# A two-layer hybrid decoder trunk: TensorE in traced order, and the weights' low parts subtracted on GpSimd

## The chip, the cores and the metric

The kernel runs on one core of one Trainium2 chip. Its time is device microseconds of one execution; the medians are of several runs. The profile is of one execution of the same program. TensorE (PE in the views) does matmuls and transposes, VectorE (DVE) and ScalarE (ACT) read and write both on-chip memories, GpSimd (POOL) works on SBUF, and SyncE (SP) issues most loads. Each engine runs its own instructions in one order; between engines they wait for each other through semaphores.

## The reference

The input `x` has 512 rows of 1024. Each of two layers normalises it, projects it with one wide matrix (1024 to 12388), runs five branches on the parts, gates each branch with a SiLU, projects each to 1024 columns, adds them under sigmoid gates and projects the sum once more:

```
xn = rms_norm(h, norm_g[l])
(a_q, a_k, a_v, i_q, i_k, i_w, b_cq, b_ckv, b_kr, c_q, c_k, c_v,
 d_u, d_v, e_q, gates, merge) = jnp.split(xn @ w_in[l], offsets, axis=-1)
branches = (dsa_branch(...), mla_branch(...), diff_branch(...), sgu_branch(...), memory_branch(...))
mixed = functools.reduce(jnp.add, [
    jax.nn.sigmoid(merge[:, :, n]) * ((o * jax.nn.silu(gates[:, :, n])) @ w_branch[l, n])
    for n, o in enumerate(branches)])
h = h + mixed @ w_out[l]
...
return rms_norm(h, final_norm_g)
```

Branch A attends to keys picked by an indexer, B is latent attention with a separate rotary key, C is differential attention (two softmaxes of half heads, one taken from the other), D is a causal spatial mixing in chunks of 128 rows after a layer norm, E attends to 256 memory rows. All is float32.

## The kernel before

**Weights.** All weights are float32 in HBM. A weight tile of 128x512 is loaded into one of four `raw` buffers by SyncE, two tiles to a load; ScalarE copies it to `wh` in a rounded type (line 374), and VectorE subtracts: `wl = raw - wh` (line 377, `split_steps`). There are 556 such tiles and five slots of `wh` and `wl`. Activations are split the same way (`split`, lines 191 and 192). Each product is then three matmuls, high by high, low by high and high by low (`three`, lines 459 to 461), so a tile of 512 columns takes twelve matmuls of 128x128 by 512.

**Order.** The program is traced by Python generators. `plan` lists the weight units in the order of a string, and between the matmuls of a unit `tick` moves on by some nanoseconds: it takes one step of splitting the next weights, and gives queued attention steps their turn when their delay has run out (`Pace`, with constants such as `LAG_QROPE` and `PACE`). What this emits is the traced order. The tile framework is called with `schedule_with_timeline_sim=True`: a scheduler then puts each engine's instructions in an order of its own, by a simulated timeline, with the traced order as priority, as long as the data dependencies hold.

**Where that order was tied by hand.** In the differential scores (`diff_attention`, line 1122) six matmuls belong together: three products for each of two halves of 64 rows. `behind` (line 180) adds a dependency without a semaphore from each to the one before it, which fixes the order of the six, but not that they stand next to one another.

**Names.** PSUM has three pools: four banks `m` (`pm` for the units, `pz` for branch D's spatial products), three banks `a` (`pa`, `pS` scores, `pT` and `pN` transposes, `pI` indexer) and one bank `o` (`po`). A bank is taken again once its last reader is done. `kh`, `kl`, `qh` and `ql` are the split keys and queries, filled by lines 191, 192 and, for the rotary rows of branch B, by copies at lines 916 and 917. `vnh` and `vnl` are the split output of the layer norm, a chain of VectorE instructions at lines 1210 to 1217. `z` (line 1239) is the activation that empties `pz`. `pth` and `ptl` are the split transposed probabilities.

**GpSimd** holds the mask and table building at the start, the small `pow` of each norm (line 250), the product of the spatial weights with the triangle (line 1184, four times) and a few loads.

Of the kernel before, what the change touches and what calls it, by code (L numbers as in the profile page):

```python
# [12 lines left out]
ALU = mybir.AluOpType  # L13
# [41 lines left out]
class Pace:  # L55


    def __init__(self):
        self.queues = {}
        self.later_ = []  # L60
        self.owner = {}
        self.now = 0.0
        self.busy = set()
# [69 lines left out]
def trunk(tc, d, out, taps=None):  # L133
    nc = tc.nc
    V, A, G, T = nc.vector, nc.scalar, nc.gpsimd, nc.tensor
    pace = Pace()
    PSUM = bass.MemoryType.PSUM
    stack = []

    def pool(name, bufs, **kw):  # L140
        p = tc.tile_pool(name=name, bufs=bufs, **kw)
        stack.append(p)
        return p.__enter__()
# [8 lines left out]
    smp = pool("small", 16)  # L152
    psp = pool("ps", 1, space=PSUM)
    drp = pool("scr", 1, space=bass.MemoryType.DRAM)
# [7 lines left out]
    def tr(dt=F32, name="tr"):  # L162
        return trp.tile([128, 512], dt, tag="tr", name=name)

    def small(n=1, name="sm"):
        return smp.tile([128, 8], F32, tag="sm", name=name)[:, :n]
# [4 lines left out]
    def psa(name="pa"):  # L171
        return psp.tile([128, 512], F32, tag="a", bufs=3, name=name)

    def pso(name="po"):
        return psp.tile([128, 512], F32, tag="o", bufs=1, name=name)

    def f32(ap):
        return ap.bitcast(F32)

    def behind(ins, prev):  # L180

        if prev is not None:
            tc.add_manual_dep(ins.ins, prev.ins.name, mybir.DependencyInfo(
                mybir.DependencyClass.NoSync, mybir.DependencyReason.DATA), reason="behind")
# [67 lines left out]
    def rstd_of(ss, n, eps, width, name="rstd"):  # L252
        r = small(n, name)
        V.tensor_scalar(r, ss, 1.0 / width, eps, op0=ALU.mult, op1=ALU.add)
        rsqrt(r, r)
        return r
# [95 lines left out]
    order, state = [], {"dma": 0, "split": 0, "slot": 0}  # L352
# [10 lines left out]
    def wtile():  # L363
        i = state["slot"] % NW
        state["slot"] += 1
        return [wp.tile([128, 512], F32R, tag=f"{n}{i}", bufs=1, name=n) for n in ("wh", "wl")]

    def split_steps(g):
        g.h, g.l = [], []
        for a in range(0, g.n, g.per):  # L370
            b = min(a + g.per, g.n)
            h, lo = (z.rearrange("p (k c) -> p k c", k=g.per) for z in wtile())
            raw, hv, lv = g.raw[:, a:b, :g.width], h[:, :b - a, :g.width], lo[:, :b - a, :g.width]
            A.activation(hv, raw, AF.Copy)  # L374
            g.h.append(h)
            yield
            V.tensor_tensor(out=lv, in0=raw, in1=f32(hv), op=ALU.subtract)  # L377
            g.l.append(lo)
            yield

# [165 lines left out]
    def softmax_head(ps, L, mask, scale):  # L546
        p = pp.tile([128, 512], F32, tag="p", name="p")
        m = small(1, "m")
        V.tensor_tensor_reduce(out=p[:, :L], in0=ps[:, :L], in1=mask, op0=ALU.add, op1=ALU.min,  # L549
                               scale=-scale, scalar=-GONE, accum_out=m)  # L550
        s = small(1, "s")
        A.activation(p[:, :L], p[:, :L], AF.Exp, bias=m, scale=-1.0, accum_out=s)  # L552
        return p, s
# [97 lines left out]
    def layer(l, mm):  # L651
# [457 lines left out]
        def diff_attention(hf):  # L1109
            sc = 64 ** -0.5  # L1110
            X = S[f"df{hf}"]

            def scores(e, i):
                L = 128 * (i + 1)
                N = max(256, L)
                q = slice(i * 128, i * 128 + 128)
                pss = [psa("pS") for _ in range(2)]
                rows = [slice(64 * s, 64 * s + 64) for s in range(2)]
                prev = None
                for n, (a, b) in enumerate(((0, 0), (0, 1), (1, 0))):  # L1120
                    for ps, r in zip(pss, rows):
                        mm = T.matmul(ps[:, :N], X["q"][e][a][r, q], X["k"][e][b][r, :N], start=n == 0, stop=n == 2)  # L1122
                        behind(mm, prev)
                        prev = mm
                return lambda: [softmax_head(ps, L, cm[:, 512 - 128 * i:640], sc) for ps in pss]

            def norm(ps_, e, i):
                L = 128 * (i + 1)
                (p0, s0), (p1, s1) = ps_
                r0, r1 = small(1, "r0"), small(1, "r1")  # L1130
                V.reciprocal(r0, s0)
                V.reciprocal(r1, s1)
                V.tensor_tensor(out=r1, in0=r1, in1=nlam[:, l:l + 1], op=ALU.mult)
                V.tensor_scalar(p1[:, :L], p1[:, :L], r1, None, op0=ALU.mult)
                V.scalar_tensor_tensor(out=p0[:, :L], in0=p0[:, :L], scalar=r0, in1=p1[:, :L],
                                       op0=ALU.mult, op1=ALU.add)

            def pv_rows(e, i):
                o = pso()
                for kb in range(i + 1):  # L1140
                    for part in range(2):
                        T.matmul(o[:, :256], pf[part][:, kb * 384 + i * 128:kb * 384 + i * 128 + 128],  # L1142
                                 X["v"][kb][:, e].rearrange("p z c -> p (z c)"),
                                 start=(kb == 0 and part == 0), stop=(kb == i and part == 1))
                on = X["o"].setdefault(e, [None] * 4)
                on[i] = rows = tr(name="don")
                A.activation(rows[:, 128:256], o[:, 128:256], AF.Copy)
                V.tensor_tensor(out=rows[:, :128], in0=o[:, :128], in1=rows[:, 128:256], op=ALU.add)
                ss = small(1, "dss")
                A.activation(rows[:, 128:256], rows[:, :128], AF.Square, accum_out=ss)  # L1150
                r = rstd_of(ss, 1, RMS_EPS, 128.0, "dr")
                V.tensor_scalar(rows[:, :128], rows[:, :128], r, None, op0=ALU.mult)

            def flip(e):
                p = psa("pN")
                for i in range(4):
                    T.transpose(p[:, i * 128:(i + 1) * 128], X["o"][e][i][:, :128], ident)
                oT["C"][2 * hf + e] = blk(F32, "oC")
                A.activation(oT["C"][2 * hf + e], p, AF.Copy, scale=dgain[:, l:l + 1])

            X["o"] = {}
            yield 2500.0
            yield from attend("C", causal_steps(range(2)), scores, norm,
                              lambda ps_, e, i: transposes(ps_[0][0], i), flip, pv_rows)

# [173 lines left out]
        for tok in ORDER.split():  # L1339
            c, a = tok[0], tok[1:]  # L1340
# [111 lines left out]
    mm = mm0 = {"rows": memt}  # L1452
    plan.append(lambda: None)
    for l in range(DEPTH):
        mm = layer(l, mm)
# [50 lines left out]
```

## Time and profile before

| | |
|---|---|
| median of 3 runs | 1822.18 us (1821.29 to 1822.37) |
| profiled execution | 1820.71 us, its span 1818.8 us |
| granted clock of TensorE | 0.993 on average |
| busy: TensorE, VectorE, ScalarE, GpSimd | 1769.3, 1158.0, 953.0, 65.7 us |
| instructions: TensorE, VectorE, ScalarE, GpSimd | 8793, 2801, 2143, 133 |

The span is from the first instruction to the last. Busy time counts work, not waiting. The list of waits of one engine says what each instruction waited for, how long in total and how often; the timeline of an engine gives the start of each instruction, its duration, and in brackets the idle time before it with what ended it. Rows of a matmul give about 0.39 us for 512 columns, though one begins about 0.23 us after another, because they overlap; the steps are therefore read from start to start.

### The profile page before, as it was taken

What the parts mean: (1) busy time and instruction counts of PE and PEld (TensorE: products, weight loads), DVE (VectorE), ACT (ScalarE), POOL (GpSimd) and SP (SyncE); (2) the same over time, 40 slices, a digit from 0 to 9 for tenths busy, and PEclk for the clock granted to TensorE, in tenths of its full rate; (3) what the DMA queues carried; (4) which work ended last, traced back from release to release, by engine and by line L of the source; (5) the groups of instructions that cost most, each with busy time, mean ns of one, the idle gap of its engine ahead of it and who ended that gap; (6) DMA issues with size and microseconds to landing.
All of it is one profiled execution on the core that took longest, in us unless ns stands there. A gap on an engine that the chain in (4) does not pass through costs nothing.

```text
span 1818.8 us, 24673 instructions
## 1 busy us (share of the span) xinstructions
PE 1769.3 (97%) x8793; PEld 1467.0 (81%) x8793; DVE 1158.0 (64%) x2801; ACT 953.0 (52%) x2143; POOL 65.7 (4%) x133
## 2 busy tenths in 40 slices
PE   7999999999989999999999999999999899999998
PEld 6877788877778888888987878788777788888887
DVE  7549776676786656445466497667767856554544
ACT  7447766444445665234355477564444556552333
POOL 1000000001010000000000000000010100000000
PEclk9999999999999999999999999999999999999999
DMA  7222221323223222343352322223232232223332
GB/s 237 76 70 62 69 77 58 94 81 100 63 81 93 79 73 82 93 126 93 121 172 58 76 62 76 82 59 93 70 104 70 59 93 70 70 84 105 113 127 70
DMA packets 151587, 161.00 MB, mean 89 GB/s; under 512 B 26293, under 2 KB 130793, under 8 KB 151465
## 3 DMA queue, kind: packets, MB, share of 16 engines
q1 hardware_dynamic: 148520, 149.21, 28.4%
q0 software_dynamic: 2944, 10.23, 1.7%
q8 instruction: 69, 1.13, 0.3%
q14 instruction: 54, 0.43, 0.1%
HBM read 155.22 MB, written 4.19 MB: 88 GB/s over the span
## 4 chain that ended last, share of the span: by engine, by line
PE 94%; DVE 4%; ACT 1%; issue 1%; DMA 0%; SPq 0%; POOL 0%; POOLq 0%; DVEq 0%; ACTq 0%
PE pm L459 27%; PE pm L460 27%; PE pm L461 27%; PE pT L567 2%; PE po L577 2%; PE pS L1122 2%; PE po L1142 1%; DVE wl L377 1%; PE pS L461 1%; PE pa L1026 1%; PE pS L460 1%; PE pS L459 1%; PE pa L532 1%; PE pS L1055 1%; PE pS L1054 1%
## 5 line engine op out<-in xcount | busy, mean ns | idle before, releaser
L377 DVE TENSOR_TENSOR wl<-raw,wh 128x512 fp32r<-128x512 f32 x556 | 376.9, 684 | 362.6 <-ACT wh L374 340.0
L374 ACT ACTIVATE wh<-raw 128x512 fp32r<-128x512 f32 x556 | 345.4, 625 | 445.9 <-PE pm L460 267.9
L459 PE MATMUL pm<-xh,wh 128*128 128x512 f32 x1040 | 414.6, 399 | 3.2 <-ACT nat L1019 2.3
L460 PE MATMUL pm<-xl,wh 128*128 128x512 f32 x1040 | 408.6, 393 | 0.0
L461 PE MATMUL pm<-xh,wl 128*128 128x512 f32 x1040 | 407.9, 393 | 0.0
L459 PEld LDWEIGHTS pm<-xh,wh 128*128 128x128 f32 x1040 | 195.9, 188 | 44.3 <-ACT nat L1019 2.7
L461 PEld LDWEIGHTS pm<-xh,wl 128*128 128x128 f32 x1040 | 195.7, 188 | 41.1 <-issue 0.7
L460 PEld LDWEIGHTS pm<-xl,wh 128*128 128x128 f32 x1040 | 195.9, 188 | 36.5 <-issue 0.5
L460 PE MATMUL pm<-wl,xh 128*128 128x512 f32 x512 | 202.0, 395 | 0.0
L461 PE MATMUL pm<-wh,xl 128*128 128x512 f32 x512 | 200.8, 394 | 0.0
L459 PE MATMUL pm<-wh,xh 128*128 128x512 f32 x512 | 200.5, 399 | 0.0
L552 ACT ACTIVATE p<-p,m 128x512 f32<-128x512 f32 (+1 forms) x192 | 107.1, 558 | 90.3 <-DVE m L549 89.9
L459 PE MATMUL pm<-yh,wh 128*128 128x512 f32 x320 | 125.5, 394 | 1.6 <-DVE acc L1311 1.6
L460 PE MATMUL pm<-yl,wh 128*128 128x512 f32 x320 | 126.2, 394 | 0.0
L461 PE MATMUL pm<-yh,wl 128*128 128x512 f32 x320 | 125.5, 393 | 0.0
L459 PEld LDWEIGHTS pm<-wh,xh 128*128 128x128 f32 x512 | 96.5, 188 | 20.3 <-ACT mth L1300 0.7
L461 PEld LDWEIGHTS pm<-wh,xl 128*128 128x128 f32 x512 | 96.4, 188 | 19.7
L460 PEld LDWEIGHTS pm<-wl,xh 128*128 128x128 f32 x512 | 96.6, 189 | 18.6 <-issue 0.5
L192 DVE TENSOR_TENSOR ptl<-pT,pth 128x512 fp32r<-128x512 f32 (+3 forms) x176 | 88.6, 504 | 30.8 <-ACT pth L191 29.7
L191 ACT ACTIVATE pth<-pT 128x512 fp32r<-128x512 f32 (+3 forms) x176 | 78.5, 448 | 53.6 <-PE po L577 33.5
L549 DVE CUSTOM_DVE_ANT_0 p<-pS,cm 128x128 f32<-128x128 f32 (+3 forms) x144 | 65.2, 464 | 50.3 <-PE pS L461 31.3
L558 ACT ACTIVATE p<-p,r 128x512 f32<-128x512 f32 (+3 forms) x128 | 71.4, 558 | 19.8 <-DVE r L557 19.3
(342 smaller groups left out, 2878.0 us busy)
## 6 DMA issues: line engine op xcount, KB each, us to landing
raw<-w_in SPq DMA_DIRECT2D x176, 512.0 KB, 3.7
raw<-w_branch SPq DMA_DIRECT2D x40, 512.0 KB, 3.5
raw<-w_in SPq DMA_DIRECT2D x36, 256.0 KB, 3.0
raw<-mem_w_kv SPq DMA_DIRECT2D x16, 512.0 KB, 4.9
raw<-w_out SPq DMA_DIRECT2D x16, 512.0 KB, 3.8
raw<-mla_w_uq SPq DMA_DIRECT2D x18, 128.0 KB, 2.7
xrow<-x SPq DMA_DIRECT2D x4, 512.0 KB, 7.3
raw<-mla_w_ukv SPq DMA_DIRECT2D x16, 128.0 KB, 2.5
```

The lines of the kernel that those rows point to most:

```text
L191: A.activation(hi, src, AF.Copy)
L192: V.tensor_tensor(out=lo, in0=src, in1=f32(hi), op=ALU.subtract)
L374: A.activation(hv, raw, AF.Copy)
L377: V.tensor_tensor(out=lv, in0=raw, in1=f32(hv), op=ALU.subtract)
L459: T.matmul(o, ah, bh, start=st, stop=False)
L460: T.matmul(o, ah, bl, start=False, stop=False)
L461: T.matmul(o, al, bh, start=False, stop=sp)
L549: V.tensor_tensor_reduce(out=p[:, :L], in0=ps[:, :L], in1=mask, op0=ALU.add, op1=ALU.min, scale=-scale, scalar=-GONE, accum_out=m)
L552: A.activation(p[:, :L], p[:, :L], AF.Exp, bias=m, scale=-1.0, accum_out=s)
L558: A.activation(p[:, :L], p[:, :L], AF.Copy, scale=r)
L567: T.transpose(ps[:, kb * 128:(kb + 1) * 128], p[:, kb * 128:(kb + 1) * 128], ident)
L577: T.matmul(o[:, q0:], v, pf[part][:, kb * 384 + q0:kb * 384 + 512], start=(kb == 0 and n == 0), stop=(kb == 3 and n == len(ts) - 1))
```

## The change

A class `InOrder` takes the place of `nc.tensor`: `matmul` and `transpose` go through it, and each instruction is given a dependency without a semaphore on the one issued before it. The scheduler can then no longer move any TensorE instruction past another: TensorE's order is the traced one. The other engines are still ordered by the scheduler. The pair order in `diff_attention` by `behind` is dropped. In `split_steps` the subtraction moves from VectorE to GpSimd; its operands are the same. In the changed file the matmuls and transposes all have the lines 152 and 155, of the class, and other lines are 21 higher.

```diff
+    class InOrder:
+        def __init__(self):
+            self.last = None
+
+        def _chain(self, ins):
+            if self.last is not None:
+                tc.add_manual_dep(ins.ins, self.last.ins.name, mybir.DependencyInfo(
+                    mybir.DependencyClass.NoSync, mybir.DependencyReason.DATA), reason="in order")
+            self.last = ins
+            return ins
+
+        def matmul(self, *a, **k):
+            return self._chain(nc.tensor.matmul(*a, **k))
+
+        def transpose(self, *a, **k):
+            return self._chain(nc.tensor.transpose(*a, **k))
+
+    T = InOrder()
...
             A.activation(hv, raw, AF.Copy)
             g.h.append(h)
             yield
-            V.tensor_tensor(out=lv, in0=raw, in1=f32(hv), op=ALU.subtract)
+            G.tensor_tensor(out=lv, in0=raw, in1=f32(hv), op=ALU.subtract)
...
-                prev = None
                 for n, (a, b) in enumerate(((0, 0), (0, 1), (1, 0))):
                     for ps, r in zip(pss, rows):
                         mm = T.matmul(ps[:, :N], X["q"][e][a][r, q], X["k"][e][b][r, :N], start=n == 0, stop=n == 2)
-                        behind(mm, prev)
-                        prev = mm
```

The number of matmuls and of vector instructions stays; 556 instructions go from VectorE's queue to GpSimd's. Three places of TensorE's order show what the chain does.

The first is the latent attention's keys in layer 1, near 178 us: `pm_1976` is the second bank of keys, `pm_2022` and `pm_2023` hold the values, and `pm_2070` and `pm_2071` are the next unit, which takes the keys' banks. TensorE before, at the first use of `pm_2071`:

```order
L461 MATMUL pm_2070<-xh4_119,wl_2080 128x512
L459 MATMUL pm_2070<-xh5_120,wh_2079 128x512
L460 MATMUL pm_2070<-xl5_128,wh_2079 128x512
L461 MATMUL pm_2070<-xh5_120,wl_2080 128x512
L459 MATMUL pm_2070<-xh6_121,wh_2092 128x512
L460 MATMUL pm_2070<-xl6_129,wh_2092 128x512
L461 MATMUL pm_2070<-xh6_121,wl_2093 128x512
L459 MATMUL pm_2071<-xh0_115,wh_2029 128x512
```

The same place now:

```order
L152 MATMUL pm_2023<-wh_1982,ckvl_1608 128x256
L152 MATMUL pm_2070<-xh0_115,wh_2029 128x512
L152 MATMUL pm_2070<-xl0_123,wh_2029 128x512
L152 MATMUL pm_2070<-xh0_115,wl_2030 128x512
L152 MATMUL pm_2071<-xh0_115,wh_2029 128x512
L152 MATMUL pm_2071<-xl0_123,wh_2029 128x512
L152 MATMUL pm_2071<-xh0_115,wl_2030 128x512
L152 MATMUL pm_2070<-xh1_116,wh_2029 128x512
```

Before, seven products of `pm_2070` (21 matmuls) came ahead of the first of `pm_2071`; now the two banks take turns, and one product (three matmuls) does.

The second is branch D's spatial products, near 543 us; `pN` is the transpose of branch C's output. TensorE before:

```order
L461 MATMUL pz_5844<-vnh_5556,wsl_5320 128x256
L460 MATMUL pz_5855<-vnl_5558,wsh_5319 128x256
L461 MATMUL pz_5855<-vnh_5556,wsl_5320 128x256
L459 MATMUL pz_5866<-vnh_5557,wsh_5336 128x256
L1157 MATMUL pN_5764<-ident_95,don_5721 128x128
```

And now:

```order
L152 MATMUL pz_5855<-vnh_5556,wsl_5320 128x256
L152 MATMUL pz_5866<-vnh_5557,wsh_5336 128x256
L152 MATMUL pz_5866<-vnl_5559,wsh_5336 128x256
L152 MATMUL pz_5866<-vnh_5557,wsl_5337 128x256
L152 MATMUL pz_5866<-vnh_5557,wsh_5336 128x256
```

The banks were begun one after another, with transposes in between; now each bank's two halves follow each other, the 24 matmuls of four banks in a row.

The third is one group of differential scores, `pS_4016` and `pS_4017`. TensorE before:

```order
L1122 MATMUL pS_4016<-kh_3732,qh_3702 128x384
L459 MATMUL pm_3962<-xh0_115,wh_3906 128x512
L460 MATMUL pm_3962<-xl0_123,wh_3906 128x512
L461 MATMUL pm_3962<-xh0_115,wl_3907 128x512
L459 MATMUL pm_3962<-xh1_116,wh_3906 128x512
```

And now:

```order
L152 MATMUL pS_4016<-kh_3732,qh_3702 128x384
L152 MATMUL pS_4017<-kh_3732,qh_3702 128x384
L152 MATMUL pS_4016<-kl_3733,qh_3702 128x384
L152 MATMUL pS_4017<-kl_3733,qh_3702 128x384
L152 MATMUL pS_4016<-kh_3732,ql_3703 128x384
L152 MATMUL pS_4017<-kh_3732,ql_3703 128x384
```

Before, the first matmul stood alone, 22 weight matmuls ahead of its five partners; now the six follow one another.

## Rows read from the trace of the kernel before

**Rows 1.** The page: busy time of each engine; then the chain by engine.
```profile
PE 1769.3 (97%) x8793; PEld 1467.0 (81%) x8793; DVE 1158.0 (64%) x2801; ACT 953.0 (52%) x2143; POOL 65.7 (4%) x133
...
PE 94%; DVE 4%; ACT 1%; issue 1%; DMA 0%; SPq 0%; POOL 0%; POOLq 0%; DVEq 0%; ACTq 0%
```

**Rows 2.** The page's groups: line, engine, operation; busy us, mean ns; idle before, releaser.
```profile
L377 DVE TENSOR_TENSOR wl<-raw,wh 128x512 fp32r<-128x512 f32 x556 | 376.9, 684 | 362.6 <-ACT wh L374 340.0
L374 ACT ACTIVATE wh<-raw 128x512 fp32r<-128x512 f32 x556 | 345.4, 625 | 445.9 <-PE pm L460 267.9
```

**Rows 3.** Waits of TensorE: waiting tile, releaser: us in total, times, longest.
```profile
PE pz L459 <- ACT vnh L191: 11.2, 2, 5.6
PE pa L231 <- DMA vec<-mla_kv_norm_g: 6.7, 1, 6.7
PE po L459 <- ACT pth L191: 3.5, 4, 1.5
PE pI L996 <- DVE iqs L969: 3.3, 2, 1.6
...
PE pm L459 <- DVE kl L192: 0.9, 1, 0.9
```

**Rows 4.** Busy us by stretch; columns: stretch, length, engines with instructions, clock, DMA.
```profile
170.00:192.00 22.00, 19.23 (x95) 15.07 (x94) 20.97 (x44) 20.68 (x43) 0.00 (x0) 1.00 0.22 55
...
530.00:553.00 23.00, 17.27 (x91) 14.96 (x90) 22.17 (x65) 14.02 (x38) 3.27 (x5) 0.85 0.20 58
```

**Rows 5.** Timeline of TensorE, near 375 and near 479: start, duration, line, instruction.
```profile
374.85 0.39 PE L460 MATMUL pm<-xl,wh 128*128 128x512 f32 x1
375.07 0.39 PE L461 MATMUL pm<-xh,wl 128*128 128x512 f32 x1
375.39 0.38 PE L1122 MATMUL pS<-kh,qh 64*128 64x256 f32 x1
375.70 0.50 PE L459 MATMUL pm<-xh,wh 128*128 128x512 f32 x1
...
479.13 0.39 PE L461 MATMUL pm<-yh,wl 128*128 128x512 f32 x1
479.45 0.38 PE L1122 MATMUL pS<-kh,qh 64*128 64x256 f32 x2
...
480.00 0.39 PE L1142 MATMUL po<-dv,pth 128*128 128x256 f32 x1
```

**Rows 6.** Timeline of GpSimd, two products that follow each other.
```profile
448.26 2.61 POOL L1184 TENSOR_TENSOR wsr<-wsr,tril 128x512 f32<-128x512 f32 x2 [3.37 <-DMA wsr<-sgu_w]
```

**Rows 7.** Timeline of VectorE in the same microseconds.
```profile
448.38 1.31 DVE L316 TENSOR_TENSOR rope<-nat,sP 128x64 f32<-128x64 f32 x1
...
449.69 0.67 DVE L1012 MATCH_REPLACE8 score<-m,score 128x512 f32<-128x512 f32 x1
450.28 0.74 DVE L318 TENSOR_TENSOR nat<-rope 128x128 f32<-128x128 f32 x1
```

**Rows 8.** Line 316, all of one shape: shortest, middle and longest in ns.
```profile
L316 DVE TENSOR_TENSOR rope<-nat,sP x24: 205/214/1306, 328.4 to 1447.5; 128x64 f32<-128x64 f32 x24
```

**Rows 9.** Timeline of ScalarE at the latent attention's keys.
```profile
182.40 0.58 ACT L191 ACTIVATE kh<-pm 64x512 fp32r<-64x512 f32 x1
183.01 0.63 ACT L916 ACTIVATE kh<-krh 32x512 fp32r<-32x512 f32 x1
...
188.31 0.62 ACT L374 ACTIVATE wh<-raw 128x512 fp32r<-128x512 f32 x1
```

**Rows 10.** Timeline of TensorE at branch D's spatial products.
```profile
542.79 0.79 PE L459 MATMUL pz<-vnh,wsh 128*128 128x256 f32 x2 [5.58 <-ACT vnh L191]
...
546.54 0.28 PE L461 MATMUL pz<-vnh,wsl 128*128 128x256 f32 x1
546.66 0.28 PE L459 MATMUL pz<-vnh,wsh 128*128 128x256 f32 x1
```

**Rows 11.** Timeline of ScalarE behind them.
```profile
544.57 1.22 ACT L1239 ACTIVATE z<-pz,cols 128x128 f32<-128x128 f32 x4 [0.80 <-PE pz L461]
```

## The prediction

> **What bounds the kernel now.** I read the engines' busy times first: TensorE is busy 1769.3 of 1818.8 us, VectorE 64%, ScalarE 52%, GpSimd 4%, and the chain of work that ended last is TensorE for 94% of its length [rows 1]. So no engine but TensorE can be shortened to any effect, and the question is only what TensorE's idle time becomes: 1818.8 - 1769.3 = 49.5 us, of which the list of its waits names 42.2 us, the sum of its 19 rows, and about 7 us lie behind its last matmul. The largest rows are few [rows 3]: 11.2 us in two waits for `vnh` ahead of the spatial matmuls of branch D, 6.7 us for a load at the start, 3.5 us for `pth`, 3.3 us for `iqs`, 0.9 us for `kl`. About 10 us of the 42 lie in the first 50 us and are not touched. The rest, some 32 us, come in a few places of each layer, where the other engines are full: in the 22 us from 170, VectorE is busy 20.97 and ScalarE 20.68 [rows 4]; in the 23 us from 530, VectorE 22.17. Elsewhere TensorE never waits.
>
> In the profiled execution 1820.71 us passed, 1.9 more than its span; the median of the runs, 1822.18, is 1.5 above it. I add changes to the profiled run and 1.5 at the end.
>
> **The differential scores become contiguous: a gain.** Six matmuls on 64 rows make up a group; two of them, on the two halves of the rows, run side by side. In a whole group of width 256, the matmul before starts at 479.13, the group at 479.45 and the next at 480.00 [rows 5]: 0.55 us for six, two at a time. In 18 of the 32 groups the scheduler leaves the first alone among the weights' matmuls and the other five later. The lone one has nothing beside it: the weight matmul before starts at 375.07, the lone one at 375.39, the next at 375.70 [rows 5]. Instead of one interval of 0.22 to 0.23 (374.85 to 375.07) there pass 0.63, so it costs 0.40, and the five left behind take as long as six do. In the new order all 32 groups stand whole: 18 x 0.40 = -7.2 us. Removing `behind` costs nothing, as the chain holds the same pairs.
>
> **VectorE loses the 556 subtractions**, 376.9 us [rows 2]. VectorE bounds nothing over the span, so this is worth only what TensorE waits for it; ScalarE's copies of 345.4 us [rows 2] stay, so of ScalarE's queue nothing goes.
>
> **GpSimd gets them.** The nearest row is its product over the same 128x512 in float32: two of them took 2.61 us, 1.31 each [rows 6]; that it writes another type here I can't see. 556 x 1.31 = 728 us, 40% of the span. It has to keep up with TensorE: a tile's twelve matmuls take 12 x 0.229 = 2.75 us, so up to twice that price GpSimd is hidden by the tile prepared ahead, and a wait for `wl` costs nothing. SyncE's raw buffers come free about 0.6 us later per tile, under four buffers; loads have that much in hand. Also the `pow` instructions and a few DMA issues of GpSimd stand behind a subtraction of at most 1.3 us; I put them at nothing beside the lags of 4 us that the source gives them.
>
> **But GpSimd and VectorE hold each other up.** While that product ran (448.26 to 449.61), a VectorE product of two SBUF inputs that takes 0.214 in the middle took 1.31, and the next one 0.74, while MATCH_REPLACE8 with one input took its usual 0.67 beside it [rows 6 to 8]. With GpSimd at work 40% of the time, such a VectorE instruction meets one under way 4 times in 10 and waits half of 1.31: 0.40 x 0.65 = 0.26 us on average. That matters where VectorE's queue is on TensorE's path, and there each layer has four places with some 15 to 20 such instructions between the event that starts the queue and the one TensorE waits for: at 0.28 each 5 us a place, 43 us in all eight; at 0.15 19 us; at nothing 0. I take 13, nearer to the low end, because the subtraction can just as well wait for VectorE, and the same queues are 40% of a subtraction shorter per tile.
>
> The Trainium skill, "SBUF — State Buffer", section "SBUF: two separate sides", says that the port pair is an exclusive lock between GpSimd and VectorE operations with two SBUF inputs, held for the whole instruction, and the loser blocks. By it every such meeting costs its full rest, which is the 43 us; rows 7 agree for two inputs and for one.
>
> **The order.** Today a scheduler moves whatever can run into TensorE's gaps. From now on a matmul that waits holds all behind it. I went through the new order and compared, for each pair of a TensorE result and the first matmul that needs its evacuation, the time of TensorE's instructions between the two (0.228 us per 512 columns [rows 5], 0.12 per 256 [rows 10]) with the sum of the queue in between. The same sum for the old order gives 48.8 us where about 43 are seen, so it leans high by some 6.
> - The MLA keys, near 178. Old: the first matmul of `pm_2071`, which needs the keys' bank, had 21 matmuls of `pm_2070`, the scores and the indexer ahead of it. New: three of `pm_1976`, 24 of 256 columns and three of `pm_2070`: 6 x 0.228 + 24 x 0.119 = 4.2 us. ScalarE has to do 13 instructions there, 4 of `kh` at 0.58, 6 copies of the rotary part at about 0.62, two weight copies at 0.62 and one more [rows 9]: 7.9 us. 3.7 us are waited where 0.9 is now [rows 3]; the rotary part of q ahead of it adds up to 2.3. Together +5 a layer.
> - The merge between 212 and 264: ScalarE's 25 instructions from a `pth` to the last `qh`, 14.6 us, over TensorE's 10.6; with smaller waits beside it +4.5 a layer.
> - Branch D, 530 to 550. Old: 5.58 us [rows 10]. The 24 spatial matmuls stood mixed with the transposes of C and A. New: in a row. A tile's second three waits for the two activations of its first half, four of which took 1.22 [rows 11]. Each of four tiles so costs 1.2 to 1.5, near 5.5; ahead of them the queue of VectorE (47 instructions, 16.4 us without subtractions) over TensorE's 13.9 and the handing over leaves 3.1. 8.6 for 6.2: +2.5.
> - The memory branch near 100: 2.4 us of matmuls now stand between `pth` and its use where 0.3 to 0.8 did: -2.1. Near 440: -1.3. The first use of `yD` near 576: +0.6.
>
> Sum: 5 + 4.5 + 2.5 - 2.1 - 1.3 + 0.6 = 9.2 a layer, 18.4 in two, 1 at the start: +19. In all +19 - 7.2 + 13 = +25; 1820.7 + 25 + 1.5 = **1847 us**. With no lock: +12; with the dear one: +55.
>
> **Rivals.**
> *The waits go* (the other side). TensorE's waits of the middle are waits for VectorE and ScalarE in queues that the weight tiles lengthen; VectorE's loses up to 0.69 of every 3.27 us. The new order is the one for which the source's lags were written, and if ScalarE runs ahead of it, it has emptied its queue when `kh` falls due: my sums, which start every queue at full length, then count waits that don't occur. For it: in the 20 us around 540 four subtractions lie in the chain to `vnh`, 2.7 us a layer. Against it: ScalarE's 20.68 of 22 us near 170 [rows 4], which lose nothing. It decides at the keys: if TensorE waits less than 1 us ahead of the second bank, it holds. Then TensorE's waits for VectorE after the start, 11 us in the nine rows of the list, and the split groups go: 1822 - 11 - 7 = 1804; if all 32 go, 1783.
> *The lock is dear.* Every exposed instruction pays 0.26 or more, and ScalarE, which waits for VectorE's results, is pushed back too: +55, 1877; if a subtraction with this output type takes over 2.75 us, GpSimd is the bound, and at 3.5 us 556 x 3.5 = 1946.
> The Trainium skill, "Perfetto Trace Analysis", section "Optimizing Scalar/DVE Operations", warns that moving work between GpSimd and VectorE may not help, since they share a port. Here it would take this rival's time; the long VectorE rows [rows 7] are on its side.
> *Nothing measurable.* Waits only change places: new ones of some 7 to 10 us are paid for by the split groups: 1819 to 1826. A difference under 0.2% (3.6 us) can't be told from none here.
>
> **How the numbers follow.** The forecast, 1832 to 1862, gets 0.46; the waits going, 1783 to 1818, 0.25; the dear lock, above 1862, 0.20; nothing measurable 0.09. Slower is 0.46 + 0.20 = 0.66. The range from 1806 to 1890 leaves out about half of the second (0.12) and the far third of the dear lock (0.07).
>
> **What would show it.** In the profile of the changed kernel: 32 whole score groups, each 0.5 to 1.0 us; the subtraction on GpSimd at 1.3 to 1.5 us from start to start; VectorE's busy time down by less than 377, as its two-input instructions are stretched (up to 150 us over 578 of them); waits of TensorE of 3 to 4 us ahead of `pm` near 185 and between the `pz` tiles, for ScalarE; hardly any wait for `wl`. Wrong would be: GpSimd at over 2.7 us a subtraction with waits for `wl` all along; no wait of TensorE at the keys; VectorE rows unstretched.

## The result: 43 us slower, and the profile after

The changed kernel takes 1865.53 us (median of 4 runs, 1864.12 to 1866.07) against 1822.28 of the kernel before beside it: 1.0238 times, with a 95% interval of 1.0226 to 1.0251. The forecast was 1847 in a range of 1806 to 1890, slower with a chance of 0.66. The direction and the range held; the size is 43 us where 25 were forecast, and the sections below show that not all of its terms were right. The profiled execution has a span of 1862.2 us, 43.3 more than before, and its mean granted clock is 0.982 (0.993 before).

The page of the changed kernel, busy time by engine and the chain by engine, answers to [rows 1]; the group of the moved subtraction to [rows 2]:

```profile
PE 1780.0 (96%) x8793; PEld 1473.8 (79%) x8793; DVE 950.7 (51%) x2245; ACT 959.1 (52%) x2141; POOL 779.4 (42%) x689
...
PE 84%; DVE 8%; ACT 4%; issue 2%; POOL 1%; DMA 1%; SPq 0%; POOLq 0%; ACTq 0%; DVEq 0%
...
L398 POOL TENSOR_TENSOR wl<-raw,wh 128x512 fp32r<-128x512 f32 x556 | 718.5, 1298 | 991.3 <-ACT wh L395 948.7
```

VectorE lost 556 instructions of 376.9 us, but its busy time fell by only 1158.0 - 950.7 = 207.3. What stayed on it takes longer, if not by the 170 us between the two numbers: part of these is overlap, since one VectorE instruction begins a little before the one ahead of it ends (449.69 and 0.67, then 450.28, in [rows 7]). Added up one by one, the 2245 instructions that stayed took 913.8 us before and take 1045.6 now, 132 us more: 85 of it in TENSOR_TENSOR, which reads two tensors, 43 in TENSOR_SCALAR, which reads one tensor and a scalar per row. The chain, 94% TensorE before, now runs for 8% over VectorE.

The waits of TensorE in the changed kernel (waiting tile, releaser: us in total, times, longest) answer to [rows 3]:

```profile
PE pa L155 <- DVE xs L546: 12.8, 8, 4.5
PE pm L152 <- DVE kl L213: 9.5, 4, 3.0
PE pz L152 <- ACT z L1257: 7.6, 8, 1.4
PE pa L155 <- DMA vec<-mla_kv_norm_g: 6.6, 1, 6.6
PE pS L152 <- DVE ptl L213: 6.2, 2, 3.1
PE pN L155 <- DVE don L1170: 5.1, 2, 2.5
PE po L152 <- DVE dr L275: 4.5, 2, 2.2
PE pa L155 <- DVE iqs L990: 4.4, 2, 2.2
PE pa L155 <- DVE meml L217: 3.0, 3, 1.4
PE pI L152 <- ACT relu L1020: 2.7, 2, 2.1
```

All 20 rows of that list sum to 74.9 us, 32.7 more than before. No row names `wl`: TensorE never waits for a low part. The other 10.7 us are in TensorE's busy time, although the whole score groups shorten it: after the waits its clock is lower. Busy us by stretch of the changed kernel (columns as in [rows 4]; the number behind the last engine is the granted clock):

```profile
160.00:170.00 10.00, 7.80 (x31) 6.64 (x32) 8.20 (x17) 5.54 (x11) 3.93 (x10) 0.66 0.18 54
200.00:210.00 10.00, 6.96 (x25) 5.45 (x24) 3.88 (x10) 5.91 (x13) 2.10 (x2) 0.66 0.11 37
```

In the first, TensorE had waited 2.2 us at 159, in the second 2.08 and 3.04 us at 197 and 200. TensorE's timeline behind the second pair, in the changed kernel:

```profile
199.41 0.47 PE L152 MATMUL pm<-xh,wh 128*128 128x512 f32 x1 [2.08 <-DVE kl L213]
...
203.38 0.77 PE L152 MATMUL pm<-xh,wh 128*128 128x512 f32 x1 [3.04 <-DVE kl L213]
203.95 0.63 PE L152 MATMUL pm<-xl,wh 128*128 128x512 f32 x1
204.37 0.63 PE L152 MATMUL pm<-xh,wl 128*128 128x512 f32 x1
```

Behind the second wait matmuls of 512 columns begin 0.42 us apart (203.95 to 204.37) instead of 0.23: the clock is at its lower level of 1.2 GHz. The same instructions in the same order, with the subtractions on VectorE (first experiment below), keep TensorE busy for 1765.6 us, 14.4 less.

### The profile page after: what moved, and what is told of

Its sections match the earlier page's. It is cut to its first block, busy times and chain, and to the rows that moved or that the text cites. A ratio compares the mean times of both kernels' runs of the same rounds, so it can differ in the third digit from the quotient of the medians.

```text
span 1862.2 us, 24850 instructions
## 1 busy us (share of the span) xinstructions
PE 1780.0 (96%) x8793; PEld 1473.8 (79%) x8793; DVE 950.7 (51%) x2245; ACT 959.1 (52%) x2141; POOL 779.4 (42%) x689
## 4 chain that ended last, share of the span: by engine, by line
PE 84%; DVE 8%; ACT 4%; issue 2%; POOL 1%; DMA 1%; SPq 0%; POOLq 0%; ACTq 0%; DVEq 0%
PE pm L152 71%; PE pS L152 4%; PE po L152 4%; PE pT L155 2%; PE pa L155 1%; DVE xs L546 1%; ACT wh L395 1%; DVE sguv L1233 1%; DVE cq L837 1%; DMA raw<-mem_w_kv 0%; ACT p L573 0%; DVE m L1032 0%; ACT z L1257 0%; DVE score L1033 0%; DVE p L740 0%
## 5 line engine op out<-in xcount | busy, mean ns | idle before, releaser
L398 POOL TENSOR_TENSOR wl<-raw,wh 128x512 fp32r<-128x512 f32 x556 | 718.5, 1298 | 991.3 <-ACT wh L395 948.7
L152 PE MATMUL pm<-xh,wh 128*128 128x512 f32 x1040 | 422.0, 406 | 11.3 <-DVE kl L213 9.5
L152 PEld LDWEIGHTS pm<-xh,wh 128*128 128x128 f32 x1040 | 196.6, 189 | 52.1 <-issue 13.2
L152 PE MATMUL pm<-wh,xh 128*128 128x512 f32 x512 | 208.6, 407 | 0.0
L1329 DVE SCALAR_TENSOR_TENSOR mth<-mth,pm 128x512 f32<-128x512 f32 x64 | 43.4, 684 | 172.8 <-PE pm L152 172.8
L152 PE MATMUL pm<-yh,wh 128*128 128x512 f32 x320 | 130.1, 407 | 0.0
```

Source lines behind the costliest of these rows:

```text
L152: return self._chain(nc.tensor.matmul(*a, **k))
L398: G.tensor_tensor(out=lv, in0=raw, in1=f32(hv), op=ALU.subtract)
L1329: V.scalar_tensor_tensor(out=dst, in0=th[m], scalar=1.0, in1=ps[m], op0=ALU.add, op1=ALU.mult)
```

## Where the time went, by stage

To compare kernels whose orders differ, I counted each matmul with its undisturbed interval (0.228 us for 512 columns, 0.172, 0.119 and 0.11 for 384, 256 and 128, half for the paired ones) and read off when the same sum of work is reached. The table gives the us that a kernel loses against the one before in each stage; negative is a gain. Names and times are of the kernel before; "1" and "2" are layers.

| stage (us before) | change | order only | GpSimd only | window locked | window + GpSimd | two windows + some GpSimd |
|---|---|---|---|---|---|---|
| start (to 34) | 9.1 | 5.7 | 5.0 | -0.1 | 4.7 | 0.4 |
| memory branch 1 (34 to 128) | -1.3 | -2.9 | 2.2 | 0.0 | 1.7 | -1.5 |
| indexer's queries 1 (to 161) | 4.8 | 2.7 | -1.5 | 0.8 | -1.5 | -1.5 |
| latent keys 1 (to 223) | 6.7 | 4.0 | -0.8 | 0.8 | -0.6 | -0.6 |
| merge 1 (to 299) | 4.1 | 4.0 | -0.2 | 0.0 | -0.3 | -0.2 |
| differential 1 (to 507) | -3.8 | -5.0 | -0.5 | -3.7 | -3.4 | -3.7 |
| branch D 1 (to 611) | 4.2 | -1.6 | -1.8 | -7.8 | -2.2 | -7.8 |
| rest 1 (to 892) | 0.8 | -0.3 | 0.1 | 0.0 | 0.1 | 0.0 |
| border (892 to 957) | 9.4 | 1.3 | 8.0 | 0.0 | 7.5 | 0.0 |
| memory branch 2 | -2.9 | -4.3 | 0.3 | -1.6 | -1.0 | -4.5 |
| indexer's queries 2 | 4.5 | 2.2 | -3.3 | -0.6 | -3.4 | -3.3 |
| latent keys 2 | 4.4 | 5.8 | 1.4 | -1.5 | 1.2 | 1.2 |
| merge 2 | 1.7 | 1.6 | -2.7 | 0.0 | -2.6 | -2.6 |
| differential 2 | -4.8 | -5.9 | -0.7 | -4.7 | -4.4 | -4.7 |
| branch D 2 | 6.2 | 0.8 | -1.9 | -7.1 | -1.0 | -7.1 |
| rest 2 | 0.3 | 0.3 | 0.0 | 0.0 | 0.0 | 0.0 |
| whole span | 43.3 | 8.4 | 3.4 | -25.6 | -5.1 | -36.1 |

Each column is one execution, and a stage varies between executions. The two border runs below differ from each other only in which of seven subtractions at the border stand on VectorE; yet the start costs 10.6 in one and 8.5 in the other, and branch D of layer 1 4.5 and 6.7. A difference of 2 us in one stage of one run is no evidence by itself.

## The experiments

Theory A stood after the result: the order and GpSimd each take a part, GpSimd above all at the start and the border, where it holds up the norm. The rivals were that one of the two does it all.

**Order only** and **GpSimd only.** The edits, each of them one half of the change:

```diff
-            G.tensor_tensor(out=lv, in0=raw, in1=f32(hv), op=ALU.subtract)
+            V.tensor_tensor(out=lv, in0=raw, in1=f32(hv), op=ALU.subtract)
```
```diff
-            V.tensor_tensor(out=lv, in0=raw, in1=f32(hv), op=ALU.subtract)
+            G.tensor_tensor(out=lv, in0=raw, in1=f32(hv), op=ALU.subtract)
```

> TensorE in traced order as in the change, but the subtractions stay on VectorE. Theory A (order and GpSimd each take a part: in the change some 18 us go at the start and at the border of the layers, where GpSimd holds up the norm, and some 25 us in the middle places by the order): 1835 to 1848 us, the start and the border within 3 us of the kernel before, the key banks and the spatial products waiting as in the change. Theory B (the order alone does it): 1860 to 1866. Theory C (GpSimd alone does it): 1815, the seven us of the score groups and nothing else.

> Subtractions on GpSimd as in the change, TensorE's order left to the scheduler as before. Theory A: 1831 to 1842 us, with the eight products xs of the norm stretched from 0.42 to 0.9 us each and the pow instructions queued behind subtractions, so that the first matmuls of both layers come some 9 us later, and little in between. Theory B: 1822, as VectorE has room. Theory C: 1860 or more.

Order only: 1829.04 us, 1.0031 times (1.0019 to 1.0043). GpSimd only: 1823.34 us, 0.9999 times (0.9990 to 1.0008). Each is below the bounds of theory A. B fails in the first run and is met in the second (1822), C fails in both: the halves cost 8.4 and 3.4 us of span, the whole 43.3. **The two halves don't add up; 31 us exist only where both are done.** The halves are not alike in all else: for GpSimd only the scheduler sorts TensorE anew too (some 1480 of its 8793 instructions stand elsewhere than before), while order only and the change have the same TensorE order, but some 170 of VectorE's 2245 other instructions and 110 of ScalarE's 2141 stand elsewhere. GpSimd only is no change in sum but not in parts: it loses 13.0 at the start and the border and gains 9.6 in sum elsewhere. In its list of waits the norm stands first:

```profile
PE pa L532 <- DVE xs L525: 10.3, 4, 5.1
```

**GpSimd's share once more, beside VectorE's.** With the order fixed and the subtractions on VectorE, GpSimd does each subtraction a second time, for nobody:

```diff
             V.tensor_tensor(out=lv, in0=raw, in1=f32(hv), op=ALU.subtract)
+            G.tensor_tensor(out=spare.rearrange("p (k c) -> p k c", k=g.per)[:, :b - a, :g.width], in0=raw, in1=f32(hv), op=ALU.subtract)
```

> TensorE in traced order and the 556 subtractions on VectorE (1829 us), and beside each the same subtraction once more on GpSimd into a buffer that nobody reads. Nothing waits for GpSimd but the raw buffers and its own pow and loads. Theory lock (GpSimd and VectorE hold each other up, and a fixed order passes it on to TensorE): 1865 or more, since VectorE keeps its own subtractions and they are held up too, with the same places longer as in the change. Rival (the change pays for low parts that come later, as TensorE or the copies wait for them): 1829 to 1835.

1922.88 us, 1.0548 times (1.0531 to 1.0566), 94 us over order only. Nothing of TensorE's needs these results. The groups on GpSimd and VectorE in that run (busy us, mean ns):

```profile
L400 POOL TENSOR_TENSOR spare<-raw,wh 128x512 fp32r<-128x512 f32 x556 | 868.9, 1563 | 889.7 <-ACT wh L396 592.5 <-issue 230.2 <-POOL spare L400 43.4
...
L399 DVE TENSOR_TENSOR wl<-raw,wh 128x512 fp32r<-128x512 f32 x556 | 543.9, 985 | 214.1 <-ACT wh L396 213.1
```

VectorE's subtraction goes from 684 [rows 2] to 985 ns, GpSimd's from 1298 in the change to 1563: each holds up the other. TensorE's list of waits names `wl` in this run no more than in the change, so a wait for low parts that come later is not what either pays for; the rival falls. TensorE's order is that of order only, and of VectorE's 2245 other instructions only some 46 stand elsewhere. The raw buffers and GpSimd's own `pow` wait for the added work too, and this run doesn't tell their parts from the lock's.

**The two edges.** The change with 19 of the 556 subtractions back on VectorE, the first nine and ten at the border of the layers:

```diff
+VSUBS = set(range(0, 9)) | set(range(278, 288))
...
-            G.tensor_tensor(out=lv, in0=raw, in1=f32(hv), op=ALU.subtract)
+            e = V if i0 in VSUBS else G
+            e.tensor_tensor(out=lv, in0=raw, in1=f32(hv), op=ALU.subtract)
```

> The change, but 19 of the 556 subtractions (the first 9, and 10 at the border of the two layers) back on VectorE. Theory A: 1847 to 1853 us, 12 to 18 less than the change, since the norm's products and the pow are free of them there. Theory B: 1865, nothing moves. Theory C (the lock costs everywhere in proportion to the subtractions): 19/556 of the loss, about 1864.

1855.19 us, 1.0174 times (1.0160 to 1.0188), 10 us less than the change. The start costs 5.4 and the border 1.3 us, what the order alone costs there (5.7 and 1.3), so 3.7 and 8.1 us of the edges were these 19 subtractions; some 5 us came back in the middle (the indexer and the keys of layer 2, branch D of layer 1), which put the sum 2 us over my bounds; the part of branch D is no larger than what two executions differ by.

The same 19 with the scheduler's order:

> Scheduler's order, subtractions on GpSimd but for 19 at the start and at the border of the layers, which go back to VectorE. With all 556 on GpSimd start and border cost 5.0 and 8.0 us and the rest gained some 9.6: 1809 to 1814 us if the two edges are free of GpSimd's subtractions only because of these 19. Rival (the scheduler's gains elsewhere come from the same shift of work, and go too): 1820 to 1824.

1811.87 us, 0.9938 times (0.9922 to 0.9955): the edges cost 0.7 and 0.0 us, and the gains elsewhere stay. 537 subtractions on GpSimd are worth 9.1 us of span to the scheduler's order.

**What GpSimd does at the border.** Here the norm of layer 2 needs a `pow` of GpSimd for each row tile, and then eight products `xs` of 128x512 on VectorE, before TensorE can transpose. VectorE and GpSimd in the changed kernel:

```profile
938.78 0.33 DVE L275 TENSOR_SCALAR rstd<-hs 128x1 f32<-128x1 f32 x4
942.54 7.34 DVE L546 TENSOR_SCALAR xs<-h,rstd 128x512 f32<-128x512 f32 x8 [3.43 <-POOL rstd L271]
```
```profile
936.35 3.80 POOL L398 TENSOR_TENSOR wl<-raw,wh 128x512 fp32r<-128x512 f32 x3 [0.38 <-ACT wh L395]
940.11 0.56 POOL L1430 DMA_DIRECT2D hscr<-h  x1
940.69 1.31 POOL L398 TENSOR_TENSOR wl<-raw,wh 128x512 fp32r<-128x512 f32 x1
941.94 2.40 POOL L271 TENSOR_TENSOR rstd<-rstd,mhalf 128x1 f32<-128x1 f32 x4
944.31 3.69 POOL L398 TENSOR_TENSOR wl<-raw,wh 128x512 fp32r<-128x512 f32 x3
```

The inputs of the `pow` are there at 939.1; it starts at 941.94, behind a subtraction, the issue of a DMA and another subtraction. Then three subtractions run beside the products: eight take 7.3 us, where before two fours took 1.67 each. It is a single one that waits out all three (shortest, middle and longest in ns):

```profile
L546 DVE TENSOR_SCALAR xs<-h,rstd x8: 473/476/4558, 942.5 to 949.4; 128x512 f32<-128x512 f32 x8
```

To tell the queue from the lock, first the products went to ScalarE:

```diff
-                V.tensor_scalar(s, half(rows[t], c), r, None, op0=ALU.mult)
+                A.activation(s, half(rows[t], c), AF.Copy, scale=r)
```

> The change, but the products xs of the two norms on 1024 columns (one input, on VectorE) are done by ScalarE. In the change the eight at the border took 0.92 us each instead of 0.42, behind subtractions on GpSimd. Theory lock: 3 to 5 us less at the border and 2 to 4 at the start, together 1857 to 1861. Rival (the border is late because the pow stands in GpSimd's queue): not over 2 us less, 1863 to 1866.

1867.65 us, 1.0244 times (1.0229 to 1.0260): no gain, a miss. At the border the loss falls by 2.1 us, to 7.3, since ScalarE needs less for the eight than VectorE beside the subtractions, though more than the 3.3 of an undisturbed VectorE; at the start 12.2 us are lost instead of 9.1:

```profile
945.42 5.01 ACT L546 ACTIVATE xs<-h,rstd 128x512 f32<-128x512 f32 x8
```

That settles nothing, since the products changed engine as well as lost their neighbours. So the change was run with the four subtractions ahead of the `pow` on VectorE, and again with the three behind them:

```diff
+VSUBS = set(range(279, 283))
```
```diff
+VSUBS = set(range(283, 286))
```

> The change, with the four subtractions that stand in GpSimd's queue just ahead of the norm's pow at the border back on VectorE, the three behind them left. If the pow's place in the queue is what is late: the four pow start 2.5 to 3.2 us sooner after their inputs and the border's loss falls from 9.4 to about 6. If only the lock on the products xs counts: 9 to 10. The whole: 1861 to 1863 or 1865.

> The change, with the three subtractions that run on GpSimd beside the norm's products xs at the border back on VectorE, the four ahead of the pow left. If the lock stretches the products: the eight take 3.4 us instead of 7.3, or the three subtractions of 2.0 us in front of or among them more, and the border's loss falls from 9.4 to 5 to 7. If only the queue counts: 9 to 10. The whole: 1861 to 1863 or 1865.

1861.79 and 1860.14 us, 1.0212 and 1.0203 times (1.0191 to 1.0232, 1.0182 to 1.0223), medians of two runs each. The border costs 5.9 and 4.9 us instead of 9.4. VectorE's products in the first and in the second of the two:

```profile
943.23 5.61 DVE L549 TENSOR_SCALAR xs<-h,rstd 128x512 f32<-128x512 f32 x8 [2.01 <-POOL rstd L272]
```
```profile
946.50 3.25 DVE L549 TENSOR_SCALAR xs<-h,rstd 128x512 f32<-128x512 f32 x8
```

The second run separates the two causes. VectorE's order is that of the change, and the `pow` is as late: it starts 3.16 us after its first input begins (942.15 to 945.31; in the change 938.78 to 941.94), where with order only it is 0.22. The eight products take 3.25 us instead of 7.34, and 4.5 us of the border's loss are gone: that is the lock. Of the 4.9 left, 1.3 are the order's; the other 3.6 I put down to the queue, in which the `pow` still stands 2.9 us longer than with order only.

The first run doesn't separate them. VectorE's input and GpSimd there:

```profile
940.88 0.33 DVE L276 TENSOR_SCALAR rstd<-hs 128x1 f32<-128x1 f32 x4
```
```profile
941.37 1.28 POOL L401 TENSOR_TENSOR wl<-raw,wh 128x512 fp32r<-128x512 f32 x1 [0.84 <-ACT wh L397]
942.63 2.70 POOL L272 TENSOR_TENSOR rstd<-rstd,mhalf 128x1 f32<-128x1 f32 x4
945.28 2.47 POOL L401 TENSOR_TENSOR wl<-raw,wh 128x512 fp32r<-128x512 f32 x2
```

The next subtraction has moved up ahead of the `pow`, which starts 1.75 us after its first input begins, 1.4 sooner where 2.5 to 3.2 were expected; and two subtractions instead of three are left behind it, so that the products take 1.7 us less. Both are in its 3.5 us. Over the three runs the longest product takes 0.48 us with no subtraction beside it, 2.82 with two and 4.56 with three: at this place one product waits out all the subtractions that follow one another.

**Locking only where the order gains.** The column of order only shows the traced order gaining in the differential attention and the memory branch and losing in most other stages. The next run is the kernel before with the chain in one window of each layer, the differential attention (the subtractions on VectorE):

```diff
+            if tok in ("+df0", "dv"):
+                do(lock(tok == "+df0"))
...
+            if self.on and self.last is not None:
+                behind(ins, self.last)
```

> The kernel before, with TensorE held to the traced order only from the start of the differential attention to the unit dv, subtractions on VectorE. Theory A: the score groups stand whole there (28 of 32, 10 before) and no other wait comes: 1815 to 1818 us, four to seven us under the kernel before. Rival: what the groups give back is taken by waits that the scheduler had filled: 1822.

1795.85 us, 0.9849 times (0.9836 to 0.9862), 20 us better than I expected. 28 of 32 score groups stand whole, as against 10 before (18 with a lone first matmul, four cut in another way), and the stage gains 3.7 and 4.7. The larger part was not foreseen: branch D gains 7.8 and 7.1, though its spatial products lie behind the window. Two lines on branch D's statistics, of the kernel before and of this run (shortest, middle and longest in ns; first and last start):

```profile
L1210 DVE BATCH_NORM_STATS2 st<-sguv x8: 675/683/685, 517.2 to 1431.4; 128x6 f32<-128x512 f32 x8
```
```profile
L1231 DVE BATCH_NORM_STATS2 st<-sguv x8: 673/682/684, 507.4 to 1405.2; 128x6 f32<-128x512 f32 x8
```

The layer norm's first statistics come at 507.4 instead of 517.2, and the products at 534.01 without a wait:

```profile
534.01 0.49 PE L150 MATMUL pz<-vnh,wsh 128*128 128x256 f32 x2
```

The 5.58 us of [rows 10] are gone in both layers, and so is the lower clock: granted in the 23 us from 530 was 0.85 [rows 4], and is 1.00 here. Over the whole span TensorE waits 12.5 us less and is busy 13.2 us less. The statistics don't come sooner because of their matmuls. ScalarE's copies of their input out of PSUM, before and in this run:

```profile
L1199 ACT ACTIVATE sguv<-pm x8: 586/598/599, 505.1 to 1411.0; 128x512 f32<-128x512 f32 x8
```
```profile
L1220 ACT ACTIVATE sguv<-pm x8: 598/598/600, 505.7 to 1395.4; 128x512 f32<-128x512 f32 x8
```

The first copy is no sooner (505.1 and 505.7). Nor do the statistics stand higher in VectorE's queue: in both kernels the same number of the differential attention's steps is ahead of them (13 sums `don` in layer 1, 29 with layer 2). But before they start 11.5 us after their input is there, in this run 1.1, in either layer: the steps ahead of them in the queue are done sooner. That these come sooner because their score groups stand whole fits, and is not shown by itself.

> Order fixed in the differential window as in the run of 1795.9 us, all subtractions on GpSimd. If GpSimd's part adds up with the order's (it cost nothing where the scheduler ordered): 1794 to 1799. If a fixed order is what makes the lock dear: the window and the spatial products behind it lose some 5 us a layer, start and border 13 as with the scheduler, other places gain a little: 1808 to 1822.

The same with all subtractions on GpSimd (the one-line edit above): 1816.38 us, 0.9964 times (0.9952 to 0.9975), 20.5 more. Its column shows that start and border cost what they do with the scheduler's order, and that branch D, behind the window, loses 5.6 and 6.1 of what it had gained, where with the scheduler's order all through GpSimd gained 1.8 and 1.9. The number is that of the second expectation, its reason only in part: inside the window, where the order is fixed, GpSimd costs 0.3 us a layer, and the 5.6 and 6.1 lie behind it, where TensorE's order is the scheduler's.

**Two windows.** The memory branch's attention was locked as well, and then 93 subtractions, of the tiles between the two windows of each layer, moved to GpSimd:

```diff
+        do(lock(True))
         do(go_mem)
...
                 fin("g" + a)
+                if a == "mem":
+                    do(lock(False))
```
```diff
+GSUBS = set(range(48, 92)) | set(range(325, 374))
...
+            e = G if i0 in GSUBS else V
```

> The kernel before with TensorE held to the traced order in two windows of each layer: the memory branch's attention, and the differential attention up to the unit dv (the second alone gave 1795.9). In the runs with the whole order fixed the memory branch took 2.9 and 4.3 us less: 1788 to 1791 us if the windows add up. Rival: the gain there came from the late start ahead of it, and nothing is left: 1796.

> The two windows held to the traced order (1791.8 us), and only 93 subtractions, those of the tiles between the two windows of each layer, on GpSimd. With the scheduler's order GpSimd gained 2.5 us a layer or more there (indexer, latent keys, merge): 1785 to 1789. Rival: the locked window before it has already given that, or the norms of the latent queries (pow) are held up there: 1792 to 1795.

1791.82 us, 0.9830 times (0.9816 to 0.9845), and **1784.58 us, 0.9788 times (0.9774 to 0.9803)**: the best version, 38 us under the kernel before and 81 under the change. The first lies a microsecond over its bounds, since in layer 1 the window gained 1.5 instead of 2.9. The second has its gain at the indexer's queries, where it takes 1.5 and 3.3 us less than before, and at the merges, less what it gives back at the keys. TensorE's waits in it sum to 20.4 us, of which a load at the start is 6.7.

## Why the prediction was right, and where it was not

- **What bounds the kernel, and GpSimd's price.** Right. TensorE waits for no low part. Two subtractions in a row begin 1.26 us apart (3.80 us for three above); 1.31 was taken from [rows 6]. VectorE's other instructions take 132 us longer; the text said up to 150. But it counted two-input instructions alone, and a third of the 132 us is in TENSOR_SCALAR with one.
- **The score groups.** Right: 32 whole ones, -3.8 and -4.8 us in the differential stages, which also hold the wait near 440; expected were 3.6 for the groups and 1.3 for the wait, in each layer.
- **The order's places.** The places were right, their sizes in the change near: latent keys +6.7 and +4.4 (5 forecast), merge +4.1 and +1.7 (4.5), memory branch -1.3 and -2.9 (-2.1), the `pz` tiles 7.6 us of waits in both layers (near 11), the wait for `don` 2.5 a layer (3.1), the score behind the merge 3.1 (4.0). At the keys the mechanism is the one forecast: the list names VectorE's `kl`, but that waits for ScalarE's `kh`, and ScalarE works without a gap from 194.2 to 203.5 us (`kl` starts at 202.54, after 1.74 us of waiting for `kh`). Of the indexer's queries I said nothing: +4.8 and +4.5, about half of it from the order (2.7 and 2.2).
- **The split between order and lock.** Wrong, and the errors cancelled. I put the order at +19 - 7.2, some 12 us, and the lock at 13. The order alone costs 8.4, of which 7 lie at the start and the border, so only 1 in the middle, where 11 were forecast (12 less one for the start): branch D, forecast at +2.5 a layer, stands at -1.6 and +0.8, for its wait for `vnh` went. GpSimd, at the same TensorE order, costs 43.3 - 8.4 = 35: 3.4 and 8.1 at the edges and 23 in the middle, 11 of them in branch D. That the total stayed in the range is luck to that extent. The step that failed is the 13 us for the lock, 0.1 us or so per exposed instruction: I took the low end "because the subtraction can just as well wait for VectorE". (By the count that gives 43 us at 0.28, 0.15 would give 23, not the 19 of the text.) And I took the meetings for chance, 4 in 10 for half a subtraction. Behind a `pow` they are no chance. The `pow` releases the VectorE instruction that needs its result, but GpSimd goes on to the subtraction queued behind it and begins it first. GpSimd and VectorE in branch D of the changed kernel:

```profile
538.35 0.55 POOL L271 TENSOR_TENSOR lr<-lr,mhalf 128x1 f32<-128x1 f32 x1 [1.30 <-DVE lr L1231]
538.87 1.29 POOL L398 TENSOR_TENSOR wl<-raw,wh 128x512 fp32r<-128x512 f32 x1
```
```profile
538.94 1.50 DVE L1233 TENSOR_SCALAR sguv<-sguv,mv,lr 128x512 f32<-128x512 f32 x1
...
546.64 1.59 DVE L1233 TENSOR_SCALAR sguv<-sguv,mv,lr 128x512 f32<-128x512 f32 x1
548.15 1.78 DVE L1235 TENSOR_TENSOR sguv<-sguv,lnb 128x512 f32<-128x512 f32 x1
```

  In the kernel before the two kinds take 0.54 and 0.68. All eight scalings of line 1233 take 1.23 to 1.59 us, where with order only, at the same TensorE order, they take 0.53 to 0.55; the eight of the latent queries' norm (`cq`, line 837) take 1.43 to 1.45 instead of 0.41 to 0.42. Each loses about 1 us, not 0.26 on average, and the text counted only instructions with two inputs.
- **The `pow`, "at nothing beside the lags".** Wrong. At the border nothing of TensorE's stands between the norm and the transposes in the traced order, so what GpSimd's queue costs shows: about 3.6 us.
- **The start and the border, +1 and 0.** Wrong: 9.1 and 9.4, together 17.5 us more than forecast, about the 18 by which the sum falls short; the other errors cancel. Of the 18.5, 7.0 are the order's and 11.5 GpSimd's. Both are the place where a norm of 1024 columns lies between the last and the first matmul. My comparison of queues with TensorE's work looked at the middle, where work lies in between.
- **What a wait costs behind it.** Left out. The sum counted waits alone; between order only (54.9 us of waits) and the change (74.9), 20.0 us of waits were added, and 14.4 us of busy time for the same instructions in the same order, with the granted clock down from 0.991 to 0.982.
- **The rivals.** "The waits go" fell at its own point, the keys (3.0 us ahead of the second bank). "The lock is dear" is nearer to what happened than the forecast: its price of 0.26 us or more per instruction, 43 us in the places it named, stands beside 23 us in the middle, and 11.5 more at the edges, which it didn't name. The Trainium skill, "Perfetto Trace Analysis", section "Optimizing Scalar/DVE Operations", has the warning that moving work between the two may not help; with the traced order it cost 35 us, with the scheduler's order nothing, and with the edges left out it gained 0.6%.

That the two halves cost more together than apart is shown (the same subtractions cost 35 us under one order and 3.4 under another). Two things stay open. The scheduler sorts VectorE and ScalarE anew in every run, so a part of the 35 may be their order and not the lock; at the border, where VectorE's order was the same, and at the scalings behind a `pow` the rows show the lock, for the rest of the middle it is argued. And that the scheduler's order is kinder because it puts other matmuls into the gaps is argued from the stages, not shown by a run of its own: that would need the old order, fixed, with the subtractions moved. Branch D speaks against it as the only reason: behind the locked window its order was the scheduler's, and GpSimd cost nearly as much there (5.6 and 6.1) as in the change (5.8 and 5.4).

## What to carry to other kernels

Don't price an order and an offload one by one when an in-order engine waits for the results: here 8 and 3 us became 43. The reading that fits best is that less waiting, or a fixed order, takes away the slack that hid the offload's contention; no run shows that by itself. Compare kernels stage by stage at equal work; a sum of zero can hide 13 us lost and 10 won, and locking the order only where it wins, with the offload only where it wins, turned 1822 us into 1785. Look first at the places with nothing in between, such as a norm ahead of the first matmul, and there at every queue that the chain passes, small instructions included. Ask what the helper engine begins at the moment it releases the chain: here it was the next subtraction, which held up the very instruction released.

## What the runs showed of the hardware

A VectorE instruction need not have two SBUF inputs to be held up by GpSimd: the products `xs` and the scaling in the layer norm have one float32 tensor in SBUF and a scalar per row, and took up to 4.56 and 1.59 us instead of 0.48 and 0.55. MATCH_REPLACE8, also with one, was not touched (0.67 us over 512 columns in both kernels). Nor were instructions that read one of their tensors from PSUM, as this pair of groups in the changed kernel shows (busy us, mean ns):

```profile
L213 DVE TENSOR_TENSOR ptl<-pT,pth 128x512 fp32r<-128x512 f32 (+3 forms) x176 | 88.8, 504 | 73.4 <-ACT pth L212 72.1
L1331 DVE TENSOR_TENSOR acc<-acc,mth 128x512 f32<-128x512 f32 x64 | 75.7, 1212 | 0.2
```

`ptl` reads `pT` from PSUM and stands at 88.6 us in the kernel before; `acc` and `mth` both lie in SBUF and took 43.7. The Trainium skill, "SBUF — State Buffer", section "SBUF: two separate sides", names both kinds, two SBUF inputs and the two-port modes of VectorE. The runs agree with it for two SBUF inputs; that `xs` and the scaling are held up they show too, but not in which mode these run. Of the 132 us by which VectorE's instructions grew, the 32 of `acc` cost little: three quarters of its instructions lie in the merges behind 611 and 1533, where no stage lost more than 0.8 us.
